# Two-layer streaming encoder on one core: the layer-2 operand ring shrunk to four tiles when attention opens, output weights loaded into the freed room, and block 0's products dealt over eight chunks

## Chip, cores, metric

One core of a Trainium2 chip runs the program. The metric is the device time of one execution in microseconds. Of the kernel before there are three timed runs and one profiled execution.

## What is computed

The reference is one step of an encoder of two layers on a prompt of 2048 tokens and a sample of 32, width 1024, in fp32. Layer 1 is a gated delta rule with a short convolution, an output projection and a layer norm. Then keys and values are projected once, and layer 2 is attention over a sliding window of three chunks of 64 tokens, with a learned sink for each of its 16 heads (four to a key head of 64):

```python
def swa_layer(x, k, v, pos, cached, w_in, sinks, w_out, ln_g, ln_b):
    proj = x @ w_in
    q = rope_partial(proj[..., :B_QW].reshape(b, l, B_Q_HEADS, B_HD), pos) * (B_HD ** -0.5)
    z = proj[..., B_QW:]
    o = cached_attention(q, k, v, sk) if cached else banded_attention(q, k, v, sk)
    out = (o * jax.nn.silu(z)) @ w_out
    return layer_norm(DN_ALPHA * x + out, ln_g, ln_b)
...
    s = jnp.einsum('bnqkgd,bnskd->bnkgqs', qb, kb)
    p = sink_softmax(s, sinks)
    o = jnp.einsum('bnkgqs,bnskd->bnqkgd', p.astype(v.dtype), vb)
```

The change concerns only the passage from the products `x @ w_in` and `x @ w_kv` to this attention.

## The kernel before

The program runs in stages: layer 1's products, the delta rule, layer 1's output, the products of layer 2 (class `P2`), and attention (class `Attention`). Every fp32 product is made of three matmuls on operands split into a high and a low part.

**Layer 2's products.** The 2080 tokens are five blocks of 416. Blocks 1 to 4 are multiplied in pairs by a seven-product scheme (`winograd`, matmuls `ps<-xs_h,w` in the trace); block 0 is multiplied plainly (`plain`, L1259 to L1277, matmuls `ps<-x_h,w`). A unit is one of q, k, v or z and an index; a plain unit has four products, each of 12 matmuls (L1232 to L1234, 128x416), whose weights are one tile `w` of 512 KB. `load` (L1205 to L1215) keeps up to RING = 12 such tiles ahead, by DMAs issued on ScalarE (ACT). After two products, ACT scales the sum out of PSUM (L1271, tile `a`), VectorE (DVE) rotates it, and SyncE (SP) stores it to a buffer in HBM: `s_bk`, `s_bv`, `s_bq`, `s_bz` (L1371, L1358).

**Attention.** `load_kv(a, z)` fetches the keys `kT` and values `vd` of chunks a to z-1 on SP (L1423, L1429: one and four DMAs). `chunk(n)` handles 64 queries in two halves. A half is: scores S (L1565), their maximum on DVE (L1440, L1441), four exponentials on ACT (L1448), the sink's exponential (L1450), the sum on DVE (L1451, L1452), a scale of P on GpSimd (POOL, L1573), six transposes (L1580), copies `pt` on ACT (L1582) and DVE (L1584), and the value product `ot` (L1586), which DVE multiplies by the gate. Queries `qs` and gates `zs` come by SP (L1546, L1547) for each second chunk. `finish` (L1455 to L1494) is the output projection of 128 tokens, 48 matmuls `po` with the output weights `wo` (L1473 to L1475) and a layer norm; `flush(keep)` lets all but `keep` of the finished pairs through it. These matmuls can stand between the steps of a half.

**The passage.** `program` runs chunks 10 to 31 and then 0 to 9. In four rounds, four plain products are written, then a chunk, then a `load_kv`. The 16 products at stake are the last four units of `sequence` (q1, q2, q3, v of block 0). When they are done the right side of SBUF, ring included, is closed, and `open_right` loads the output weights, 8 MB in 16 DMAs of 512 KB on SP (L955). Up to the end of `P2`'s large part the order on the engines is written out by hand; in the attention the framework's scheduler chooses it from the dependences. An engine runs its own list strictly in that order. The build hands each DMA of SP and of ACT one of eight completion counters (DMAHW0 to DMAHW7) in turn, and the issuing engine waits until the previous DMA with that counter has landed.

Of the kernel before, what the change touches and what calls it, by code (L numbers as in the profile page):

```python
# [10 lines left out]
F32 = mybir.dt.float32  # L11
F32R = mybir.dt.float32r
# [7 lines left out]
D = 1024  # L20
# [137 lines left out]
def drain(gen):  # L158
    for _ in gen:
        pass  # L160
# [926 lines left out]
class P2:  # L1087
# [10 lines left out]
    def __init__(self, tc, right, mid, I, O, T, G):  # L1098
        self.tc, self.nc, self.I, self.O, self.T, self.G = tc, tc.nc, I, O, T, G
        self.res = new_pool(tc, right, "p2_res", 1, side="right")  # L1100
        self.wp = new_pool(tc, right, "p2_w", self.RING, side="right")
        self.wk = new_pool(tc, right, "p2_wk", 3, side="right")
        self.stg = new_pool(tc, mid, "p2_stg", 3, side="right")
        self.ppr = new_pool(tc, right, "p2_psr", 2, PSUM, side="right")
        self.ppl = None
        self.turn = 0
        self.todo, self.second, self.staged = [], [], []
# [99 lines left out]
    def load(self, most=2):  # L1207

        for _ in range(most):
            if self.loads and len(self.held) < self.RING:  # L1210
                what, slot = self.loads.pop(0)
                w = self.wp.tile([128, 2, 4, 128], F32R, tag="w", name="w")
                src = self.T["w2"][UNITS.index(what[:2]), SLOTS.index(slot)]
                self.nc.scalar.dma_start(w[:].rearrange("p s k c -> p s (k c)").bitcast(F32), src)
                self.held.append((what, slot, w))  # L1215

    def weight(self, what, slot):
        whose, which, w = self.held.pop(0)
# [160 lines left out]
class Attention:  # L1379


    def __init__(self, tc, left, I, O, T, G):
        self.tc, self.nc, self.I, self.O, self.T, self.G = tc, tc.nc, I, O, T, G
        nc, V = tc.nc, tc.nc.vector
        L = "left"
        self.one = one = new_pool(tc, left, "t_one", 1, side=L)
        self.two = new_pool(tc, left, "t_two", 2, side=L)
        self.thr = new_pool(tc, left, "t_thr", 3, side=L)
        self.ps_s = [new_pool(tc, left, "t_ps", 1, PSUM, side=L)]
        self.ps_t = new_pool(tc, left, "t_pt", 2, PSUM, side=L)  # L1390
        self.ps_o = new_pool(tc, left, "t_po", 1, PSUM, side=L)
        self.turn = 0
        self.kT = one.tile([128, 2, NP], F32, tag="kT", name="kT")

        self.vd = one.tile([128, 32, 2, 128], F32, tag="vd", name="vd")
        self.nsk = one.tile([128, 8], F32, tag="nsk", name="nsk")
        self.sks = one.tile([128, 4], F32, tag="sks", name="sks")
        for i in range(2):
            nc.sync.dma_start(self.nsk[i * 64:i * 64 + 64, :], I["sinks"][i].partition_broadcast(64))
        for i in range(4):  # L1400
            nc.sync.dma_start(self.sks[i * 32:i * 32 + 32, :], I["sinks_s"][i].partition_broadcast(32))
        V.tensor_scalar(out=self.nsk[:], in0=self.nsk[:], scalar1=-1.0, scalar2=None, op0=ALU.mult)
        V.tensor_scalar(out=self.sks[:], in0=self.sks[:], scalar1=-1.0, scalar2=None, op0=ALU.mult)
        self.pend = []
        self.data = {}

    def open_right(self, right):
        tc, I = self.tc, self.I
        R = "right"
        self.oone = new_pool(tc, right, "u_one", 1, side=R)  # L1410
        self.otwo = new_pool(tc, right, "u_two", 2, side=R)
        self.pp = new_pool(tc, right, "u_pp", 1, PSUM, side=R)
        self.ps_s.append(new_pool(tc, right, "u_ps", 1, PSUM, side=R))
        rest = load_out_weights(self.nc, self.oone, self.T["wo"][1])
        self.w = next(rest)
        drain(rest)

    def tables(self):
        self.tabs = ln_tables(self.nc, self.oone, self.I["b_ln_g"], self.I["b_ln_b"])
# [196 lines left out]
def program(tc, I, O, T, G):  # L1616
    nc = tc.nc
    left, right, mid = ExitStack(), ExitStack(), ExitStack()
# [51 lines left out]
    pairs = [("v", 0), ("z", 0), ("k", 0), ("z", 1), ("q", 0), ("z", 2), ("q", 1), ("z", 3), ("q", 2), ("q", 3)]  # L1670
    sequence = [("z", j, 0) for j in range(3)] + [p + (1,) for p in pairs]
    sequence += [("z", 3, 0), ("k", 0, 0), ("q", 0, 0)] + [p + (2,) for p in pairs]
    sequence += [("q", j, 0) for j in range(1, 4)] + [("v", 0, 0)]
    first, second = Filler(gated()), Filler(outputs())

    def done(ch):
# [24 lines left out]
    p2.ppl = None  # L1701
    left.close()
    mid.close()
    att = Attention(tc, left, I, O, T, G)
    att.load_kv(8, 14)
    order = list(range(10, 32)) + list(range(10))
    for i in range(4):
        drain(itertools.islice(late, 4))
        att.chunk(order.pop(0))
        if i != 2:  # L1710
            att.load_kv(*{0: (14, 18), 1: (18, 24), 3: (24, 32)}[i])
    drain(late)
    p2.rest()
    right.close()
    att.open_right(right)
    att.load_kv(0, 8)
    for n in order:
        att.chunk(n)
        if n == 15:
            att.tables()  # L1720
        if n == order[-1]:
            att.flush(1)
            att.pend.insert(0, None)
            att.pend.pop(0)
            att.sample()
            att.pend.reverse()
        if n % 2 == 1:
            att.flush(3 if n < 24 and n > 9 else 2)
# [142 lines left out]
```

## Time and profile before

| | us |
|---|---|
| profiled execution | 2252.59 (span 2250.8) |
| timed runs | 2246.57, 2263.61, 2265.81 (median 2263.61) |
| last Winograd matmul starts | 1805.8 |
| first keys issued | 1813.31 |
| first scores start | 1824.43 |
| output weights issued | 1841.9 to 1859.9 |
| first output product starts | 1881.1 |
| granted TensorE clock, mean | 0.979 |

Times are from the start of the span. In the views, PE is TensorE's matmul, PEld its weight load, and a name with a q behind it (SPq, ACTq) is an engine's queue of DMA issues. `[7.30 <-DMA w<-s_w]` behind a row says that the engine had been idle 7.30 us and what ended that. A row of the table by stretch gives start and end, length, busy time and count of each engine, the granted clock, the share of the DMA engines and GB/s.

### The profile page before, as it was taken

What the parts mean: (1) busy time and instruction counts of PE and PEld (TensorE: products, weight loads), DVE (VectorE), ACT (ScalarE), POOL (GpSimd) and SP (SyncE); (2) the same over time, 40 slices, a digit from 0 to 9 for tenths busy, and PEclk for the clock granted to TensorE, in tenths of its full rate; (3) what the DMA queues carried; (4) which work ended last, traced back from release to release, by engine and by line L of the source; (5) the groups of instructions that cost most, each with busy time, mean ns of one, the idle gap of its engine ahead of it and who ended that gap; (6) DMA issues with size and microseconds to landing.
All of it is one profiled execution on the core that took longest, in us unless ns stands there. A gap on an engine that the chain in (4) does not pass through costs nothing. (4 is left out here: it accounts for less than half of the span.)

```text
span 2250.8 us, 37045 instructions
## 1 busy us (share of the span) xinstructions
PE 2152.2 (96%) x13370; PEld 1959.0 (87%) x13370; DVE 1470.4 (65%) x2701; ACT 902.7 (40%) x2331; POOL 740.9 (33%) x1193
## 2 busy tenths in 40 slices
PE   8999999999999999999889999899989998999997
PEld 6899999999998889988777787899989986888775
DVE  4798777876484577777655665545844566556662
ACT  4555555444332466656552211311311135444441
POOL 1213111251112387777661210000000024656563
PEclk9999999999999899999999999999999999999999
DMA  7656656567734334435724874888788896233321
GB/s 285 211 185 194 193 179 197 183 193 235 235 117 130 113 117 138 148 114 171 277 75 157 285 224 148 284 279 290 249 297 291 266 286 183 85 104 94 85 80 43
DMA packets 344919, 417.40 MB, mean 185 GB/s; under 512 B 77968, under 2 KB 275696, under 8 KB 344720
## 3 DMA queue, kind: packets, MB, share of 16 engines
q1 hardware_dynamic: 312432, 314.41, 44.1%
q10 hardware_dynamic: 32304, 100.62, 13.4%
q8 instruction: 106, 1.74, 0.3%
q14 instruction: 77, 0.63, 0.1%
HBM read 265.26 MB, written 150.05 MB: 185 GB/s over the span
## 5 line engine op out<-in xcount | busy, mean ns | idle before, releaser
L77 PE MATMUL ps<-act_hi,w_hi 128*128 128x416 f32 x1280 | 459.3, 359 | 6.4 <-ACT R L297 4.3
L79 PE MATMUL ps<-act_hi,w_lo 128*128 128x416 f32 x1280 | 451.7, 354 | 5.2 <-POOL w_lo L54 5.2
L78 PE MATMUL ps<-act_lo,w_hi 128*128 128x416 f32 x1280 | 451.8, 353 | 0.0
L77 PEld LDWEIGHTS ps<-act_hi,w_hi 128*128 128x128 f32 x1280 | 242.4, 189 | 11.2 <-ACT R L297 4.6
L79 PEld LDWEIGHTS ps<-act_hi,w_lo 128*128 128x128 f32 x1280 | 242.7, 190 | 9.7 <-POOL w_lo L54 6.3
L78 PEld LDWEIGHTS ps<-act_lo,w_hi 128*128 128x128 f32 x1280 | 243.2, 190 | 2.7
L54 POOL TENSOR_TENSOR w_lo<-w_raw,w_hi 128x1024 fp32r<-128x1024 f32 x40 | 101.5, 2537 | 381.5 <-ACT w_hi L53 374.9
L1232 PE MATMUL ps<-xs_h,w 128*128 128x416 f32 x560 | 199.4, 356 | 10.9 <-DVE ra L1289 6.9
L1233 PE MATMUL ps<-xs_l,w 128*128 128x416 f32 x560 | 199.9, 357 | 2.9 <-DVE xs_l L1135 2.9
L1234 PE MATMUL ps<-xs_h,w 128*128 128x416 f32 x560 | 198.2, 354 | 0.0
L266 DVE SCALAR_TENSOR_TENSOR y<-R,convw,y 128x2083 f32<-128x2083 f32 x72 | 171.2, 2379 | 24.5 <-ACT y L264 24.4
L559 POOL TENSOR_TENSOR tm<-L,Tt 128x60 f32<-128x60 f32 (+19 forms) x375 | 132.1, 352 | 86.3 <-DVE tm L559 34.1
L562 POOL TENSOR_TENSOR Tt<-Tt,tm 128x60 f32<-128x60 f32 (+19 forms) x375 | 143.4, 382 | 28.5
L1573 POOL TENSOR_TENSOR P<-P,sm 128x384 f32<-128x384 f32 (+2 forms) x128 | 101.0, 810 | 122.5 <-DVE sm L1452 59.1
L1427 POOL MEMSET vd<- 64x768 f32 (+2 forms) x10 | 7.8, 779 | 395.9 <-DVE ra L1289 395.6
L1448 ACT ACTIVATE P<-S,nm 128x192 f32<-128x192 f32 (+2 forms) x260 | 104.8, 419 | 61.4 <-DVE nm L1441 48.9
L1232 PEld LDWEIGHTS ps<-xs_h,w 128*128 128x128 f32 x560 | 106.3, 190 | 13.8 <-DVE ra L1289 7.6
L1289 DVE SCALAR_TENSOR_TENSOR ra<-ps,u 128x416 f32<-128x416 f32 x60 | 35.4, 590 | 122.0 <-PE ps L1234 121.2
L1008 PE MATMUL po<-wo,g_hi 128*128 128x512 f32 (+1 forms) x272 | 110.5, 406 | 3.0 <-DVE r L1013 1.8
L1010 PE MATMUL po<-wo,g_lo 128*128 128x512 f32 (+1 forms) x272 | 107.5, 395 | 4.5 <-DVE g_lo L995 4.5
L1233 PEld LDWEIGHTS ps<-xs_l,w 128*128 128x128 f32 x560 | 106.1, 189 | 5.5 <-DVE xs_l L1135 4.2
L1234 PEld LDWEIGHTS ps<-xs_h,w 128*128 128x128 f32 x560 | 106.9, 191 | 1.2
(292 smaller groups left out, 4808.7 us busy)
## 6 DMA issues: line engine op xcount, KB each, us to landing
w<-s_w ACTq DMA_DIRECT2D x180, 512.0 KB
s_w<-pre_hl SPq DMA_DIRECT2D x160, 256.0 KB
w_raw<-in_w_in SPq DMA_DIRECT2D x40, 512.0 KB
s_wo<-pre_hl SPq DMA_DIRECT2D x64, 256.0 KB
wo<-s_wo SPq DMA_DIRECT2D x32, 512.0 KB
gb<-s_gcum SPq DMA_DIRECT2D x34, 256.0 KB
k<-s_k SPq DMA_DIRECT2D x34, 256.0 KB
s_z<-z SPq DMA_DIRECT2D x40, 208.0 KB
```

The source lines that it names most:

```text
L77: nc.tensor.matmul(ps, hi[:, k, :], xh[:, k, :], start=(k == 0), stop=False)
L78: nc.tensor.matmul(ps, hi[:, k, :], xl[:, k, :], start=False, stop=False)
L79: nc.tensor.matmul(ps, lo[:, k, :], xh[:, k, :], start=False, stop=(k == KC - 1))
L266: nc.vector.scalar_tensor_tensor(out=y[:], in0=R[:, j:j + W], scalar=self.convw[:, i, j:j + 1], in1=y[:], op0=ALU.mult, op1=ALU.add)
L559: P.tensor_tensor(out=tm[:n, i0 - k:, :w], in0=L[:n, i0:, j:j + 1].to_broadcast(sh), in1=Tt[:n, j:j + 1, :w].to_broadcast(sh), op=ALU.mult)
L562: P.tensor_tensor(out=Tt[:n, i0:, :w], in0=Tt[:n, i0:, :w], in1=tm[:n, i0 - k:, :w], op=ALU.subtract)
L1008: nc.tensor.matmul(ps[:n], ghi[:, k, :n], w[0][k][:, cs], start=(k == 0), stop=False)
L1010: nc.tensor.matmul(ps[:n], glo[:, k, :n], w[0][k][:, cs], start=False, stop=(k == KC - 1))
L1232: nc.tensor.matmul(ps, w[:, 0, k], xh[:], start=first and k == 0, stop=False, skip_group_check=True)
L1233: nc.tensor.matmul(ps, w[:, 0, k], xl[:], start=False, stop=False, skip_group_check=True)
L1234: nc.tensor.matmul(ps, w[:, 1, k], xh[:], start=False, stop=last and k == 3, skip_group_check=True)
L1448: nc.scalar.activation(P[u], src, AF.Exp, bias=nm[:, u:u + 1], scale=1.0, accum_out=sm[:, u:u + 1])
```

## The change

The pools of `P2` swap places, so that the ring is the last opened and can be closed alone. When the Winograd part is over, `smaller` closes the ring of 12 and opens one of 4. The four tail units are no longer in `sequence`: they start behind that, by `p2.units(tail)`, whose first step loads four tiles. The output weights are now eight tiles of 1 MB. Seven go into a new pool `t_w` of the left side, one written after each of the first seven chunks; the eighth comes with `open_right`. Eight rounds of a chunk, an output weight, two plain products and (in rounds 0, 1 and 3) a `load_kv` take the place of four rounds. The layer-norm tables are loaded behind `open_right` instead of behind chunk 15, and `flush(3)` is called once before chunk 18.

```diff
@@ class P2
-        self.wp = new_pool(tc, right, "p2_w", self.RING, side="right")
         self.wk = new_pool(tc, right, "p2_wk", 3, side="right")
+        self.ring = ExitStack()
+        self.wp = new_pool(tc, self.ring, "p2_w", self.RING, side="right")
...
+    def smaller(self, right):
+
+        assert not self.held and not self.loads
+        self.ring.close()
+        self.RING = 4
+        self.wp = new_pool(self.tc, right, "p2_w4", self.RING, side="right")
@@ class Attention
+        self.wpool = new_pool(tc, left, "t_w", 1, side=L)
+        self.wo = []
...
-        rest = load_out_weights(self.nc, self.oone, self.T["wo"][1])
-        self.w = next(rest)
-        drain(rest)
+        self.out_weight(self.oone)
+        self.w = [[w[:, s] for w in self.wo] for s in range(2)]
+
+    def out_weight(self, pool):
+
+        k = len(self.wo)
+        w = pool.tile([128, 2, D], F32R, tag=f"wo{k}", name="wo")
+        self.nc.sync.dma_start(w[:].bitcast(F32), self.T["wo"][1, k])
+        self.wo.append(w)
@@ program
-    sequence += [("q", j, 0) for j in range(1, 4)] + [("v", 0, 0)]
+    tail = [("q", j, 0) for j in range(1, 4)] + [("v", 0, 0)]
...
+    p2.smaller(right)
     att = Attention(tc, left, I, O, T, G)
     att.load_kv(8, 14)
+    late = p2.units(tail)
+    next(late)
     order = list(range(10, 32)) + list(range(10))
-    for i in range(4):
-        drain(itertools.islice(late, 4))
+    for i in range(8):
         att.chunk(order.pop(0))
-        if i != 2:
+        if i < 7:
+            att.out_weight(att.wpool)
+        drain(itertools.islice(late, 2))
+        if i in (0, 1, 3):
             att.load_kv(*{0: (14, 18), 1: (18, 24), 3: (24, 32)}[i])
     drain(late)
     p2.rest()
     right.close()
     att.open_right(right)
+    att.tables()
     att.load_kv(0, 8)
+    att.flush(3)
     for n in order:
         att.chunk(n)
-        if n == 15:
-            att.tables()
```

Up to the end of the Winograd part the engines run the same lists, except that block 0's 38 early plain matmuls are gone from PE. Three places behind it differ in what the prediction speaks of. In the rows, the number behind a name is the tile's, and the bracket lists what the instruction waits for: the counters above, and the engines' own semaphores.

ACT, where the plain products end and the softmax begins. Before:

```order
L1214 DMA w_17760<-s_w2_73 128x1024 [waits DMAHW2_49,PE_49]
L1271 ACTIVATE a_17745<-ps_17716 128x416 [waits DMAHW6_49,DVE_49]
L1214 DMA w_17778<-s_w2_73 128x1024 [waits DMAHW4_49,PE_49]
L1271 ACTIVATE a_17780<-ps_17747 128x416 [waits DMAHW1_49,DVE_49]
L1271 ACTIVATE a_17899<-ps_17870 128x416 [waits DMAHW3_49,DVE_49,PE_49]
L1271 ACTIVATE a_17932<-ps_17903 128x416 [waits DMAHW1_49,DVE_49,PE_49]
L1271 ACTIVATE a_18045<-ps_18016 128x416 [waits DMAHW1_49,DVE_49,PE_49]
L1448 ACTIVATE P_17796,sm_17800<-S_17791,nm_17797 128x3x64 [waits DVE_49,PE_49]
```

and with the change:

```order
L1215 DMA w_17932<-s_w2_73 128x1024 [waits DMAHW7_49,DMAHW2_49,PE_49]
L1279 ACTIVATE a_17934<-ps_17901 128x416 [waits DVE_49]
L1215 DMA w_18039<-s_w2_73 128x1024 [waits DMAHW3_49,DMAHW0_49,PE_49]
L1464 ACTIVATE P_17719,sm_17723<-S_17714,nm_17720 128x3x64 [waits DVE_49,PE_49]
L1464 ACTIVATE P_17719,sm_17723<-S_17714,nm_17720 128x3x64 x3
L1466 ACTIVATE es_17724<-es_17724 128x4 [waits DVE_49]
L1215 DMA w_18057<-s_w2_73 128x1024 [waits DMAHW5_49,PE_49]
L1279 ACTIVATE a_18059<-ps_18026 128x416
L1215 DMA w_18151<-s_w2_73 128x1024 [waits DMAHW6_49,DMAHW1_49,PE_49]
L1598 COPY pt_17735<-tr_17736 128x384 [waits PE_49]
```

The last weight load (`w_17778`) stood ahead of every exponential. Now the ninth weight (`w_18039`) stands ahead of the first one, the tenth and eleventh (`w_18057`, `w_18151`) ahead of the first copy `pt`. The counter DMAHW3 that the ninth waits for was last given to the sixteenth `vd` on SP, DMAHW5 of the tenth and DMAHW6 of the eleventh to the sixth and seventh output tiles.

SP, where the first output tiles and the first keys go out, with the change:

```order
L1431 DMA wo_17786<-s_wo_74 128x2048 [waits DMAHW4_49]
L1379 DMA s_bq_69<-ra_17602 128x416 [waits DMAHW5_49,DVE_49]
L1431 DMA wo_17899<-s_wo_74 128x2048 [waits DMAHW7_49]
L1431 DMA wo_18024<-s_wo_74 128x2048 [waits DMAHW1_49]
L1379 DMA s_bq_69<-ra_17557 128x416 [waits DMAHW3_49,DVE_49]
L1431 DMA wo_18136<-s_wo_74 128x2048 [waits DMAHW4_49,PE_49]
...
L1439 DMA kT_17677<-s_bk_71 128x2x384 [waits DMAHW4_49,PE_49]
```

Before, the row ahead of that `kT` was a load of the sinks, and every `wo` stood behind the last keys. Now four tiles stand ahead of the first keys: the fourth waits, by DMAHW4, for the first to land, and `kT`, by the same counter, for the fourth.

SP, behind the last of the values that the eight rounds fetch, with the change:

```order
L1445 DMA vd_17678<-s_bv_72 64x8x64 [waits DMAHW2_49]
L1445 DMA vd_17678<-s_bv_72 64x8x64 [waits DMAHW3_49]
L1431 DMA wo_18261<-s_wo_74 128x2048 [waits DMAHW4_49]
L1431 DMA wo_18373<-s_wo_74 128x2048 [waits DMAHW5_49,PE_49]
L1431 DMA wo_18491<-s_wo_74 128x2048 [waits DMAHW6_49]
L1439 DMA kT_17677<-s_bk_71 128x2x512 [waits DMAHW7_49]
```

Before, the store of a query block and then this `kT` followed on the values. Now the fifth, sixth and seventh output tiles stand between.

## Prediction

> **What bounds the kernel now.** I read the page first, then the table by stretch, because a share over the whole span hides where an engine idles.
>
> ```profile
> span 2250.8 us, 37045 instructions
> PE 2152.2 (96%) x13370; PEld 1959.0 (87%) x13370; DVE 1470.4 (65%) x2701; ACT 902.7 (40%) x2331; POOL 740.9 (33%) x1193
> ```
> ```profile
> core 0: us, PE busy (x) PEld busy (x) DVE busy (x) ACT busy (x) POOL busy (x), PEclk, DMA share, GB/s
> 1806.00:1841.00 35.00, 35.00 (x200) 32.96 (x199) 23.36 (x56) 9.14 (x32) 9.90 (x13) 1.00 1.00 245
> 1841.00:1881.00 40.00, 29.38 (x162) 21.52 (x161) 23.10 (x56) 19.77 (x85) 12.99 (x17) 0.87 1.04 327
> 1886.00:2200.00 314.00, 313.55 (x1715) 249.29 (x1714) 192.33 (x462) 145.20 (x559) 186.92 (x175) 1.00 0.30 85
> ```
> TensorE (PE) bounds the program. It is full while block 0's products fill it (1806 to 1841) and again once output products fill it (from 1886); between, some nine halves of chunks run with nothing beside them, and PE idles 40.00 - 29.38 = 10.6 us at a granted clock of 0.87 (29.38 us of work at 0.87 is worth 25.6 at full clock, 3.8 lost; at the most 40 x 0.13 = 5.2). So about 16 us is all that this change can win here, and 16 of 2252.6 is 0.7%. What releases the output products, by the view of the tile `wo` and the waits:
>
> ```profile
> L955 SPq DMA_DIRECT2D wo<-s_wo x16: 319/320/580, 1841.9 to 1859.9; - x16
> L1473 PE MATMUL po<-wo,g_hi x13: 388/392/775, 1881.1 to 1898.0; 128*128 128x512 f32 x13
> its engine sat idle before it (us, times) until:
>   issue: 0.7, 2
>   DVE pt L1584: 0.2, 1
> ```
> ```profile
> POOL P L1573 <- DVE sm L1452: 29.9, 7, 8.0
> ACT P L1448 <- DVE nm L1441: 13.1, 5, 3.9
> PE S L1565 <- ACT P L1448: 7.6, 5, 2.5
> ```
> The output weights are issued until 1859.9 and the first output product starts at 1881.1, and nothing waits for them there. The bare halves wait on themselves: scores, maximum (DVE), exponential (ACT), scale (POOL), transposes.
>
> **The change part by part.** *Work moved out of the Winograd part.* By the order on PE, 38 of the 192 matmuls of the 16 products stand before the last Winograd matmul now, and none afterwards.
>
> ```profile
> L1234 PE MATMUL ps<-xs_h,w x68: 348/352/355, 1760.2 to 1805.8; 128*128 128x416 f32 x68
> L1232 PEld LDWEIGHTS ps<-x_h,w x14: 186/188/188, 1778.1 to 1805.9; 128*128 128x128 f32 x14
> ```
> A matmul goes at the pace of its weight load, 0.188 us, so a product of 12 takes 2.26 us and the Winograd part ends 38 x 0.188 = 7.1 us sooner, at 1798.6. PE's work up to the first output product is the same 192 matmuls and 12 scores.
>
> *Weights of the tail.* Each product loads one 512 KB tile. Now the last load is issued at 1808.02 (below), before any exponential; afterwards four go out as the Winograd part ends and twelve in turn, each behind a product, on ACT's queue among the exponentials. On SP four 1 MB output tiles go out ahead of the first keys, and three behind the keys of chunks 24 to 31, ahead of those of chunks 0 to 7. The order shows each DMA waiting for one of eight counters that SP and ACT share, that is, for an earlier DMA to land. That such a wait holds the engine, the trace shows:
>
> ```profile
> 1798.75 7.71 ACTq L1214 DMA_DIRECT2D w<-s_w  x5
> 1806.56 0.52 ACT L1271 ACTIVATE a<-ps 128x416 f32<-128x416 f32 x1 [7.30 <-DMA w<-s_w]
> 1808.02 0.33 ACTq L1214 DMA_DIRECT2D w<-s_w  x1
> ```
> ```profile
> SPq L955 <- DMA wo<-s_wo: 9.0, 9, 1.6
> ACT vb L1356 <- DMA s_bv<-va: 3.7, 1, 3.7
> ```
> ACT stood 7.30 us behind the landing of a weight, and SP 9.0 us in nine waits behind its own tiles. (The Trainium skill, "DMA: Bandwidth & Descriptors", section "Anatomy of one DMA — SWDGE (gpsimd) path", says that DMA engines wait on no semaphore and the wait stands on the issuing sequencer; these rows agree. Were the wait held in the queue instead, ACT would go on to its exponentials and the sum would be that of the first rival.)
>
> *First keys.* `kT` of the first chunks waits for the fourth output tile, which waits for the first. The Winograd part's end lets the first three go at about 1796.5 (their place on SP is that of the stores that start at 1800.12 now, less what of the 7.1 us lies before them).
>
> ```profile
> 1800.12 7.84 SPq L1371 DMA_DIRECT2D s_bq<-ra  x3
> 1813.31 0.39 SPq L1423 DMA_DIRECT2D kT<-s_bk  x1
> 1813.80 2.64 SPq L1429 DMA_DIRECT2D vd<-s_bv  x4
> 1817.14 1.16 SPq L1546 DMA_DIRECT2D qs<-s_bq  x2
> 1833.30 3.41 SPq L1429 DMA_DIRECT2D vd<-s_bv  x4
> 1841.86 1.29 SPq L955 DMA_DIRECT2D wo<-s_wo  x3
> ```
> ```profile
> 1849.00:1865.00 16.00, 11.72 (x64) 8.59 (x63) 9.99 (x24) 6.95 (x32) 5.23 (x7) 0.89 1.03 407
> ```
> Four tiles (4.2 MB), five weights (2.6 MB) and three stores (0.6 MB) are 7.4 MB; at the 407 GB/s of 1849 to 1865, when tiles were loading, 18.2 us: the first keys are issued at about 1815 (at the 327 GB/s of the whole stretch 1841 to 1881, 22.6 us and 1819). Now it is 1813.31, but PE had products until then. Queries go out 3.8 to 5 us after the keys and land by the 3.7 us of `vb`'s row, so the first scores can start at about 1823, while PE has finished the five products ahead of them at 1798.6 + 5 x 2.26 = 1809.9. That idles PE 13 us.
>
> *Exponentials behind the ninth weight.* On ACT the ninth weight stands ahead of the first exponential and waits, by its counter, for the sixteenth `vd`. In the rows above that last `vd` is issued 1836.71 - 1813.31 = 23.4 us after the first keys, and 3.7 us more land it: 27 us, so 1815 + 27 = 1842. The bounds: 28 transfers at the 0.39 us of `kT` plus 3.7 is 15 us (1830); 28.5 us from first keys to first `wo` plus 3.7 is 32 (1847). I take 27, since the same 28 instructions gave it. Behind the ninth weight wait the softmax of the first half, the tenth weight (for the sixth output tile) and the eleventh (for the seventh), and behind that the first `pt` copy, for which PE waits with `ot`. The three output tiles go out at about 1840: 3.1 MB and a weight at 407 GB/s are 9 us, landing included 3.7: 1849 to 1853; I take 1851.5 for PE's restart. By then it has done seven products and two scores and one set of transposes.
>
> *What is left then*, with prices from the chain and the time line:
>
> ```profile
> 1909.86 1.29 PE ot L1586 x6
> 1911.16 0.66 PE tr L1580 x6
> 1911.81 0.85 PE S L1565 x8
> ```
> ```profile
> 1837.70 0.60 PE L1354 MATMUL ps<-ident,a 128*128 128x128 f32 x4
> 1858.49 1.61 POOL L1573 TENSOR_TENSOR P<-P,sm 128x384 f32<-128x384 f32 x2 [3.09 <-DVE sm L1452]
> 1863.08 1.61 POOL L1573 TENSOR_TENSOR P<-P,sm 128x384 f32<-128x384 f32 x2 [2.98 <-DVE sm L1452]
> ```
> Nine products 9 x 2.26 = 20.3, ten scores 8.5, nine transposes 5.9, ten `ot` 12.9, two value transposes 1.2: 48.8 us. A half is 1.29 + 0.66 + 0.85 = 2.8 us of PE and a bare one comes each 1863.08 - 1858.49 = 4.6, so 1.8 is lost in each; six or seven remain bare (nine now): 11.7. The first output product would start at 1851.5 + 60.5 = 1912, against 1881.1. It stands one transpose and two `ot` later in the order than now, 0.66 + 2 x 1.29 = 3.2 us of work already done: 1912 - 1881.1 - 3.2 = +27.7, so **+28 us**. From there PE has 313.55 of 314 us in work and the same work in both, so the delay stays to the end. The two table loads, which move ahead, cost nothing, since SP has no other load that PE waits for by then; uncovered they are
>
> ```profile
> ln_g<-in_b_ln_g SPq DMA_DIRECT2D x1, 512.0 KB
> ```
> twice 512 KB, 2.6 us at 407 GB/s.
>
> The profiled execution took 2252.6 us (span 2250.8), so its time would be 2280.6. The three timed runs lie at 2246.6, 2263.6 and 2265.8; the mean of these and the profiled one is 2257, and with +28 I forecast **2285 us**, 0.9% above the median shown.
>
> **The rivals.** *The room pays (on the other side).* If the `vd` landed before the first scores were needed, or the counters came round in another state, ACT would not be held. PE's work from 1798.6: 16 products 36.2, twelve scores 10.2, ten transposes 6.6, ten `ot` 12.9, value transposes 1.2 are 67.1, plus 11.7 for bare halves: 1877.4, less 3.2: -7 us, **2250**. It decides if the first queries land by 1810 and the sixteenth `vd` within a product or two after, which asks for the keys 13 us sooner than 7.4 MB allow; 407 GB/s against it is strong. For it speaks only that the counter's turn is taken from the build, and the landing of a tile from a rate.
> *Only the keys are late.* The ninth weight goes out early, since the `vd` are quick (15 us) and PE is idle until 1823 in any case: -7 + 13 = +6, **2263**. Against it: with 15 us after 1815 ACT is still held until 1830.
> *Longer and colder.* At 289 GB/s instead of 407
>
> ```profile
> GB/s 298 302 268 175 81 248 231 254 275 238 282 286 222 257 237 309 275 188 274 317 212 334 348 412 391 413 415 386 418 419 415 389 293 110 232 337 250 274 215 281
> DMA packets 27800, 21.68 MB, mean 289 GB/s; under 512 B 17414, under 2 KB 24658, under 8 KB 27794
> 1881.00:1886.00 5.00, 5.00 (x22) 3.57 (x21) 4.20 (x7) 3.39 (x17) 5.00 (x3) 0.67 1.15 304
> ```
> the mean of 1806 to 1881, the 7.4 MB take 25.6 us (7.4 later) and the last three tiles 3.6 later: +39, **2296**. The granted clock of 0.67 after PE's idling (1881 to 1886) adds 5 x 0.33 = 1.7 us per long gap. (The Trainium skill, "TensorE: Matmul & The Clock Gate", Part 1, halves the clock after an idle window of about 3.4 us and restores it after as long a busy one, an estimate of 1.7 us a gap; the 0.67 agrees, and two gaps would make +31 of +28.)
> *The change does not do what it says.* Room for the output weights is opened before attention, but the eighth tile still waits for the ring's end and three more stand behind the keys of chunks 24 to 31. Since no output product waited for `wo` in the rows above, that moves neither sum; it only means that nothing repays the delay.
>
> **How the numbers follow.** About 1%, 22.6 us, is what a measurement of this kernel can tell from no change. The forecast (+28, on its own +16 to +37 by the bounds of the `vd`, of the rate and of the bare halves) has 0.60; the room pays 0.15; only the keys 0.12; longer and colder 0.13. Slower by over 1% is 0.7 of the forecast's 0.60 and all of the last: 0.55; faster by over 1% asks for more than the whole 16 us and gets 0.03; the rest, 0.42, is within 1%. Range: 2256 (nearly down to the room paying) to 2306 (longer and colder, with 10 us for the spread of runs).
>
> **What would show it.** Right: the first `kT` issued at 1813 to 1821, PE idle before the first scores; ACT with a weight load on its queue that waits from about 1812 to 1842 and no exponential before; PE idle over 20 us in 1810 to 1852, bare halves six or seven; first output product at 1905 to 1920, and 313 to 314 busy of 314 us behind it. Wrong: exponentials before 1835, or a first output product before 1890, which would leave the first rival; or a tail of the program that is not full, which would let the delay be won back.

## Result and the profile after

| | before | change |
|---|---|---|
| median, us | 2260.48 (4 runs, 2246.57 to 2265.81) | 2307.14 (4 runs, 2303.38 to 2317.72) |
| profiled execution, us (span) | 2252.59 (2250.8) | 2303.38 (2301.6) |
| ratio of the times | | 1.0236, 95% interval 1.0206 to 1.0266 |

The change makes the kernel 2.4% slower, some 47 to 53 us (difference of the medians; 0.0236 of 2257). The forecast was +28 us, with 2306 as the upper end of the range. The ratios in this document leave out three single executions of 3499.79 to 4223.98 us, far above all others; one of them is the only profiled execution of the last experiment, so no row of that one is used.

To compare the two executions they must start together. The first Winograd matmul of before, then of the change (instruction, count, duration in ns, first and last start in us):

```profile
L1232 PE MATMUL ps<-xs_h,w x560: 349/352/714, 1428.9 to 1805.4; 128*128 128x416 f32 x187
```
```profile
L1240 PE MATMUL ps<-xs_h,w x560: 345/348/716, 1434.0 to 1803.8; 128*128 128x416 f32 x187
```

The change is 5.1 us late there, so 45.7 of the 50.8 us of span arise behind that point. Below, times of the change less 5.1 are put beside those of before. Of the 5.1 us, 4.1 belong to the change as well: from the last `op<-Sp,q` matmul of the delta rule (L711, at 1207.7 and 1208.7) to the first Winograd matmul it is 221.2 us before and 225.3 with the change. The swapped pools show in between: the first weight tile of layer 2 is issued 15 us behind that `op` instead of 18, and this is so in every trace with the swapped pools (eleven, with the experiments below) and in none of the five with the old ones. Layer 1's output then waits longer for its own load `r`. Waits from 1225 to 1262 us (who waited for whom: us in total, times, longest), before and then the change:

```profile
PE po L1008 <- DVE r L1013: 1.8, 1, 1.8
DVE r L1013 <- DMA r<-in_x: 0.7, 1, 0.7
```
```profile
PE po L1008 <- DVE r L1013: 4.4, 2, 2.6
DVE r L1013 <- DMA r<-in_x: 4.8, 1, 4.8
```

Over all traces the way from that `op` to the first Winograd matmul is 225.1 to 227.9 us with the swapped pools and 221.2 to 225.6 with the old ones. That the earlier weight loads delay `r` fits these rows, but no run swaps the pools alone.

The table by stretch of the change, with the header of the one before:

```profile
1804.40:1833.00 28.60, 15.52 (x61) 14.12 (x59) 6.82 (x15) 0.52 (x1) 6.32 (x9) 0.72 0.97 313
1833.00:1863.00 30.00, 11.33 (x48) 9.52 (x48) 7.58 (x21) 3.68 (x15) 1.61 (x2) 0.64 1.11 318
1863.00:1927.00 64.00, 55.76 (x311) 44.30 (x309) 29.75 (x81) 26.04 (x109) 14.95 (x19) 0.97 0.47 143
1932.00:1996.00 64.00, 62.46 (x312) 48.42 (x313) 36.87 (x74) 23.75 (x87) 32.70 (x30) 0.97 0.30 85
```

In the first 58.6 us behind the Winograd part PE works 26.85 us and idles 31.8, at a granted clock of 0.72 and 0.64. Before, the first 35 us of that place had no idle time. ACT's row of time shows who was late (start, duration, instruction; in brackets the idle time ahead and its end; an ACTq row of several issues lasts from the first to the last of them, waits included):

```profile
1800.05 28.06 ACTq L1215 DMA_DIRECT2D w<-s_w  x6
1828.21 0.52 ACT L1279 ACTIVATE a<-ps 128x416 f32<-128x416 f32 x1 [27.70 <-DMA vd<-s_bv]
1829.46 8.63 ACTq L1215 DMA_DIRECT2D w<-s_w  x2
1838.13 0.52 ACT L1279 ACTIVATE a<-ps 128x416 f32<-128x416 f32 x1 [9.40 <-DMA vd<-s_bv]
1852.83 0.33 ACTq L1215 DMA_DIRECT2D w<-s_w  x1
1853.26 0.42 ACT L1464 ACTIVATE P<-S,nm 128x192 f32<-128x192 f32 x1 [14.61 <-DMA vd<-s_bv]
1858.22 0.33 ACTq L1215 DMA_DIRECT2D w<-s_w  x1
1858.59 0.52 ACT L1279 ACTIVATE a<-ps 128x416 f32<-128x416 f32 x1 [3.53 <-DMA wo<-s_wo]
1861.80 0.33 ACTq L1215 DMA_DIRECT2D w<-s_w  x1
1862.17 0.48 ACT L1598 COPY pt<-tr 128x384 f32<-128x384 f32 x1 [3.06 <-PE tr L1596]
```

ACT does almost nothing from 1800.5 to 1853. Its first six weight loads take 28.06 us; in narrower windows they go out like this:

```profile
1800.05 1.29 ACTq L1215 DMA_DIRECT2D w<-s_w  x3
1807.54 0.33 ACTq L1215 DMA_DIRECT2D w<-s_w  x1
1821.73 0.33 ACTq L1215 DMA_DIRECT2D w<-s_w  x1
1827.78 0.33 ACTq L1215 DMA_DIRECT2D w<-s_w  x1
```

So ACT stands from the fifth weight on: 13.8 us until, by the trace's semaphore events, a load of the sinks (`sks`) has landed, which SP issues behind the fourth output tile, and the sixth weight 5.6 us more until a `vd` has. The eighth waits for a `vd` again, and the ninth until 1852.83, for the sixteenth `vd`. Everything behind stands: the drains of the products (`a`), and the exponentials. The tenth weight goes when an output tile has landed (the `wo` in brackets). SP at the same time:

```profile
1801.75 0.70 SPq L1431 DMA_DIRECT2D wo<-s_wo  x1
1804.43 0.98 SPq L1431 DMA_DIRECT2D wo<-s_wo  x2
1809.87 0.32 SPq L1431 DMA_DIRECT2D wo<-s_wo  x1
1820.85 0.40 SPq L1439 DMA_DIRECT2D kT<-s_bk  x1
1835.10 0.34 SPq L1379 DMA_DIRECT2D s_bq<-a  x1
1843.48 1.11 SPq L1379 DMA_DIRECT2D s_bq<-a  x1
1845.11 2.61 SPq L1445 DMA_DIRECT2D vd<-s_bv  x4
1847.77 2.59 SPq L1431 DMA_DIRECT2D wo<-s_wo  x3
```

Four output tiles, then the first keys at 1820.85. Two stores of the products (`s_bq<-a`) stand between the keys and values. ACT drains these products late (1828.21 and 1838.13), but SP did not wait for that: DVE is done with them at 1831.1 and 1841.2, 4.0 and 2.3 us before the stores go out. SP's waits from 1832 to 1840 us are for its own transfers:

```profile
SPq L1379 <- DMA zs<-s_bz: 2.4, 1, 2.4
SPq L1445 <- DMA kT<-s_bk: 1.3, 1, 1.3
```

PE:

```profile
1816.42 0.72 PE L1240 MATMUL ps<-x_h,w 128*128 128x416 f32 x1 [5.11 <-DMA w<-s_w]
1828.78 0.72 PE L1240 MATMUL ps<-x_h,w 128*128 128x416 f32 x1 [7.97 <-ACT a L1279]
1833.24 1.35 PE L1581 MATMUL S<-kT,qs 64*128 64x192 f32 x8
1855.03 1.65 PE L1581 MATMUL S<-kT,qs 64*128 64x192 f32 x8 [17.99 <-ACT P L1464]
1862.70 1.56 PE L1602 MATMUL ot<-pt,vd 128*128 128x256 f32 x6 [0.68 <-ACT pt L1598]
```

It waited 5.11 us for a weight, 7.97 for a drain and 17.99 for the first exponential, which frees the only bank of scores. The matmul behind the first two waits took 0.72 us and not the 0.35 of the rows around it. The granted clock behind the three waits is 0.5 for 4.1, 5.4 and 6.5 us of renewed work (until 1820.5, 1834.2 and 1861.5). (The Trainium skill, "TensorE: Matmul & The Clock Gate", Part 1, says that an idle array falls to half its clock and gets it back after at least one busy window of some 3.4 us; the 0.72 against 0.35 agrees with the half, and the three times are one to two such windows.) The first output product of the change:

```profile
L1489 PE MATMUL po<-wo,g_hi x23: 389/393/628, 1927.0 to 1959.8; 128*128 128x512 f32 x23
```

### The profile page after: what moved, and what is told of

It is laid out like the page before. It is cut to its first block, busy times and chain, and to the rows that moved or that the text cites. A ratio compares the mean times of both kernels' runs of the same rounds, so it can differ in the third digit from the quotient of the medians.

```text
span 2301.6 us, 37032 instructions
## 1 busy us (share of the span) xinstructions
PE 2165.5 (94%) x13370; PEld 1964.8 (85%) x13370; DVE 1473.9 (64%) x2701; ACT 904.3 (39%) x2331; POOL 744.1 (32%) x1193
## 3 DMA queue, kind: packets, MB, share of 16 engines
q10 hardware_dynamic: 32304, 100.62, 13.1%
## 5 line engine op out<-in xcount | busy, mean ns | idle before, releaser
L1240 PE MATMUL ps<-xs_h,w 128*128 128x416 f32 x560 | 198.9, 355 | 11.7 <-DVE ra L1297 7.7
L1240 PEld LDWEIGHTS ps<-xs_h,w 128*128 128x128 f32 x560 | 106.5, 190 | 15.3 <-DVE ra L1297 8.4
L1602 PE MATMUL ot<-pt,vd 128*128 128x256 f32 x372 | 100.3, 393 | 7.7 <-DVE pt L1600 4.7
```

What stands on the lines that cost most here:

```text
L1240: nc.tensor.matmul(ps, w[:, 0, k], xh[:], start=first and k == 0, stop=False, skip_group_check=True)
L1602: nc.tensor.matmul(ot[:, p], self.vd[:, kc0 + j, p, :], pt[:, 2 * j:2 * j + 2, :], start=(j == 0), stop=(j == nj - 1))
```

## Experiments

All ratios are to the kernel before, run on the same chip. "Scores" and "output" are the start of the first scores and of the first output product, counted from the first Winograd matmul of the same execution.

| run | ratio (95%) | scores | output |
|---|---|---|---|
| before | 1 | 395.5 | 452.2 |
| the change | 1.0236 (1.0206 to 1.0266) | 399.2 | 493.0 |
| e1_late_wo | 1.0153 (1.0110 to 1.0195) | 391.5 | 489.6 |
| e2_pool_w | 1.0129 (1.0088 to 1.0171) | 403.8 | 474.4 |
| e3_both | 1.0058 (1.0035 to 1.0081) | 390.0 | 478.0 |
| e4_deal | 1.0062 (1.0040 to 1.0084) | 397.0 | 437.4 |
| e5_tables | 0.9997 (0.9966 to 1.0028) | 396.5 | 445.4 |
| e6_nodeal | 1.0253 (1.0211 to 1.0296) | 397.7 | 494.2 |
| e7_nodeal_free | 1.0095 (1.0061 to 1.0130) | 390.2 | 468.1 |
| e8_deal6 | 1.0022 (0.9997 to 1.0047) | 396.8 | 455.0 |
| e9_ring8 | 1.0142 (1.0102 to 1.0182) | 423.6 | 463.3 |
| e10_ring8_keep | 1.0073 (1.0046 to 1.0100) | 412.6 | 461.4 |
| e11_ring12_keep | 1.0028 (1.0008 to 1.0047) | 402.5 | 442.2 |
| e12_before_wo_pool | 1.0050 (1.0027 to 1.0072) | 397.0 | 455.9 |
| e13_ring8_pool | 1.0084 (1.0052 to 1.0116) | 405.9 | 459.2 |
| e14_ring8_keep_pool | 1.0044 (1.0021 to 1.0066) | 397.3 | 453.1 |
| e15_ring12_keep_pool | 0.9995 (0.9974 to 1.0016) | | |

**Undoing one hold at a time.** The theory after the result: two holds, the first keys behind four output tiles, and ACT behind weight loads. Rival A: the ring of four is too short in itself. Rival B: the keys alone. Rival C: the dealing.

`e1_late_wo`, the seven output tiles pinned behind the last values:

```diff
@@ load_kv
-                nc.sync.dma_start(self.vd[rows, a:z, p, rows], src[:, a:z, p, rows])
+                self.last = nc.sync.dma_start(self.vd[rows, a:z, p, rows], src[:, a:z, p, rows])
@@ program
-        if i < 7:
-            att.out_weight(att.wpool)
...
+    with tc.issue_after(att.last.ins):
+        for _ in range(7):
+            att.out_weight(att.wpool)
     drain(late)
```

> The change with one thing put back: the seven output tiles go out on SP behind the last keys and values of the eight rounds instead of four of them ahead of the first keys. The ring of four and its loads on ACT stay. Theory (two holds: the first keys stand behind four output tiles, and ACT stands with a weight load behind a counter that a late transfer of SP must give back): the first hold is gone and the second shorter, since the values land some 10 us sooner; first keys at 1808 to 1813, first exponential 1825 to 1840, time 2260 to 2285, so over half of the 47 us is won back. Rival A (the short ring alone costs it: each weight is fetched too late): 2295 to 2310. Rival B (the keys alone): 2252 to 2262.

It took 2295.88 us, less than half of the loss back, so the theory's number failed, and rival B with it; it lies at the lower edge of rival A's range, which the next runs tell apart. The trace shows why, in ACT's and PE's rows of this run:

```profile
1834.88 0.42 ACT L1464 ACTIVATE P<-S,nm 128x192 f32<-128x192 f32 x1 [0.79 <-DVE nm L1457]
1878.09 0.33 ACTq L1215 DMA_DIRECT2D w<-s_w  x1
1878.46 0.52 ACT L1279 ACTIVATE a<-ps 128x416 f32<-128x416 f32 x1 [17.05 <-DMA wo<-s_wo]
```
```profile
1880.65 1.65 PE L1581 MATMUL S<-kT,qs 64*128 64x192 f32 x8 [16.58 <-ACT P L1464]
```

The first exponential came early (395.9 us from the first Winograd matmul, 419.3 in the change), but now the last weight load waited 17.05 us for an output tile to land, and the exponentials behind it with PE for 16.58 us. The hold on ACT had not gone; it had moved to where the output tiles were put.

`e2_pool_w`, the weights of the tail by GpSimd, whose transfers have counters of their own in the order:

```diff
@@ load
-                self.nc.scalar.dma_start(w[:].rearrange("p s k c -> p s (k c)").bitcast(F32), src)
+                self.queue.dma_start(w[:].rearrange("p s k c -> p s (k c)").bitcast(F32), src)
@@ __init__
         self.ring = ExitStack()
+        self.queue = self.nc.scalar
@@ smaller
         self.RING = 4
+        self.queue = self.nc.gpsimd
```

> The change with one thing put back: the sixteen weight loads of the tail are issued by GpSimd, whose transfers have counters of their own, so ACT holds no transfer among its exponentials. Four output tiles still stand ahead of the first keys. Theory: the first exponential follows the first scores within 3 us (about 1835), the 20 us in which ACT stood are gone, the late keys stay: 2265 to 2285. Rival B (the keys alone): no gain, 2300 to 2310. Rival A (short ring): no gain, 2295 to 2310.

2289.18 us: four us outside the theory's range, but neither rival's. The exponential follows on the scores by 2.9 us (406.7 against 403.8). The run is not the clean half that was meant: in its order all seven output tiles go out ahead of the first keys and not four, so the keys come at 396.6 us (386.8 in the change), and the gain by GpSimd is, if anything, understated:

```profile
1800.47 0.44 SPq L1433 DMA_DIRECT2D wo<-s_wo  x1
1803.15 2.23 SPq L1433 DMA_DIRECT2D wo<-s_wo  x4
1806.55 3.40 SPq L1433 DMA_DIRECT2D wo<-s_wo  x2
```

What is left shows mainly in one row, PE's wait for the queries that follow the late keys:

```profile
1837.77 1.65 PE L1583 MATMUL S<-kT,qs 64*128 64x192 f32 x8 [25.46 <-DMA qs<-s_bq]
```

`e3_both` joins the two edits.

> Both of the above at once: weights of the tail by GpSimd, output tiles behind the last keys. Theory: both holds are gone; within 10 us of the kernel before, 2250 to 2270. Rival A (short ring): 2285 to 2310, since each weight is still fetched only four ahead.

2274.66 us, so 0.0058 of the 0.0236, some 13 us, stay: the theory's number fails by 5 us and something of rival A is there. One wait is most of it, in PE's row (the swapped pools, too, are still in this run):

```profile
1829.12 1.65 PE L1583 MATMUL S<-kT,qs 64*128 64x192 f32 x8 [10.63 <-DMA qs<-s_bq]
```

The order of this run puts four products (48 matmuls) ahead of the first scores, where before 98 stood there; keys, then queries, still need their 13 us (377.1 to 390.0), and PE, with none of its 16 products in the Winograd part, is through with these four 10.63 us sooner.

**The other parts alone.** `e4_deal`: the kernel before with the eight rounds.

```diff
-    for i in range(4):
-        drain(itertools.islice(late, 4))
+    for i in range(8):
         att.chunk(order.pop(0))
-        if i != 2:
+        drain(itertools.islice(late, 2))
+        if i in (0, 1, 3):
...
     att.open_right(right)
+    att.tables()
     att.load_kv(0, 8)
+    att.flush(3)
...
-        if n == 15:
-            att.tables()
```

> The kernel before with the dealing alone: ring of 12, block 0's tail in the sequence, output weights as before in sixteen transfers by the open right side, but eight rounds of a chunk and two products instead of four of four products and a chunk, and the tables and one flush placed as in the change. Theory: the dealing costs nothing by itself: 2252 to 2268. Rival C (the dealing spreads products so that the halves of the chunks get less cover and the later order is worse): 2285 to 2310.

2273.48 us, beyond the theory's range and short of the rival's. The first output product came 14.8 us sooner than before, and the way from there to the end is 27.5 us longer (397.2 against 369.7), part of which is work that the kernel before does ahead of its first output product (1970 matmuls stand behind that product here, 1908 before). 9.5 us of it are idle time of PE: 397.20 - 375.58 = 21.6 against 12.1.

`e5_tables`, the tables' place alone:

```diff
     att.open_right(right)
+    att.tables()
     att.load_kv(0, 8)
...
-        if n == 15:
-            att.tables()
```

> The kernel before with the tables alone placed as in the change (loaded behind the output weights instead of behind chunk 15); ring, weights and four rounds as before. By the order this alone makes the scheduler cut the later part finer (three transposes, then output products, where six stood together). Theory D (part of the 15 us that remained with both holds gone is this finer order): 2264 to 2275, with the first output product within 5 us of before and the loss behind it. Rival C (the dealing itself): 2253 to 2263.

2257.63 us against 2256.91, the other range: theory D fell. The first output product came 6.8 us sooner and the rest took 7.3 us more. The scheduler's finer order of the later part, which this run has, costs nothing that could be measured.

`e6_nodeal`, the change with four rounds of four products ahead of a chunk and no early flush; `e7_nodeal_free`, the same with the edits of e1 and e2:

```diff
-    for i in range(8):
+    for i in range(4):
+        drain(itertools.islice(late, 4))
         att.chunk(order.pop(0))
-        if i < 7:
+        for _ in range(2 if i < 3 else 1):
             att.out_weight(att.wpool)
-        drain(itertools.islice(late, 2))
-        if i in (0, 1, 3):
+        if i != 2:
...
-    att.flush(3)
```

> The change without the dealing: ring of four, weights on ACT, output tiles by SP early, but four rounds of four products and a chunk, and no early flush. Theory (two holds, 32 us, and some 15 us by the dealing and the later order): the holds stay, so 2285 to 2305, and the first exponential stays some 20 us behind the first scores. Rival C (the dealing is what makes the holds): 2255 to 2270.

> The change without the dealing and with both holds taken away: ring of four, its weights by GpSimd, output tiles behind the last keys, four rounds of four products and a chunk, no early flush. By the order the later part is cut as in the kernel before. Theory: nothing is left that costs, 2250 to 2266. Rival A (the short ring): 2270 to 2290.

Without the dealing the holds are as large as with it, 2313.16 us (8 above the range), and the first exponential comes 27.4 us behind the first scores: rival C is out as their cause. The second missed: 2279.1, in rival A's range. Its PE has the same wait as e3's ahead of the first scores:

```profile
1832.83 1.65 PE L1583 MATMUL S<-kT,qs 64*128 64x192 f32 x8 [10.90 <-DMA qs<-s_bq]
```

`e8_deal6`: the kernel before with 3, 3, 3, 3, 2, 2 products behind six chunks.

> The kernel before with the 16 products dealt over six chunks (3, 3, 3, 3, 2, 2), ring of 12 and output weights as before, no early flush, tables behind the output weights. If the dealing itself is good for cover (a first output product 15 us earlier was seen with eight) and the flush is what costs: 2245 to 2258. Theory D (the finer later order eats it): 2262 to 2278.

2261.18 us, within a few us of before, on neither range's side: the first output product is not sooner (455.0) and nothing is won.

**A longer ring.** Here the ring that `smaller` opens is 8 or 12, and fewer output tiles go early, so that both fit:

```diff
-        self.RING = 4
+        self.RING = 8
...
-        if i < 7:
+        if i < 4:
             att.out_weight(att.wpool)
...
-        self.out_weight(self.oone)
+        while len(self.wo) < 8:
+            self.out_weight(self.oone)
```

> The change with two sizes altered: a ring of eight tiles instead of four, and four early output tiles of 1 MB instead of seven; the other four go out when the right side opens. By the order all sixteen weight loads on ACT then stand ahead of the first exponential and ten products instead of five ahead of the first scores; the four output tiles still stand ahead of the first keys. Theory (three terms: the cover that the short ring takes from the first scores, the late keys, ACT held among its exponentials): the first and third go, the late keys stay and are mostly covered by ten products (22 us): 2258 to 2275. If the late keys cost 14 us by themselves whatever stands ahead: 2272 to 2282. If only the dealing over eight chunks is left: 2268 to 2278.

2300.13 us: every expectation missed. No exponential stands behind a weight load any more, and ten products stand ahead of the scores; but ACT's drains of those products stand behind the loads:

```profile
1809.09 27.01 ACTq L1215 DMA_DIRECT2D w<-s_w  x9
1836.22 0.52 ACT L1279 ACTIVATE a<-ps 128x416 f32<-128x416 f32 x1 [26.62 <-DMA sks<-in_sinks_s]
```
```profile
PE ps L1240 <- ACT a L1279: 18.5, 3, 8.1
```

Of the waits of PE in this stretch, 18.5 us are for drains. The `sks` in brackets is the small load of the sinks behind the output tiles on SP. `e10_ring8_keep` pins each early tile in its written place, behind the first keys:

```diff
-        self.nc.sync.dma_start(w[:].bitcast(F32), self.T["wo"][1, k])
+        self.tc.keep_in_program_order(self.nc.sync.dma_start(w[:].bitcast(F32), self.T["wo"][1, k]))
```

> As the run before, but the four early output tiles keep their written places on SP, behind the first keys and between the later ones. Theory: none of the three terms is left; it stands at what the dealing over eight chunks with the ring of 12 gave (2273) or a little below, 2255 to 2273. If the keys' place costs nothing once there is cover, the same as the run before.

2280.26 us, 20 below the run before, and 7 above the range: the drains still stand behind weights, for 11.0 us instead of 18.5:

```profile
PE ps L1240 <- ACT a L1279: 11.0, 3, 5.8
```

`e11_ring12_keep`, with a ring of twelve and three early tiles:

> Ring of twelve (closed and opened again, so without the early prefetch), three early output tiles in their written places, the rest when the right side opens; eight rounds. Tells whether more room for the ring than eight is worth anything: theory, twelve products ahead of the first scores are more than are needed, the same as with eight within 8 us, 2255 to 2273.

2266.07 us, 14 below the ring of eight, more than the 8 expected.

`e12_before_wo_pool`, the sixteen output-weight loads of the kernel before on GpSimd's queue instead of SP's:

```diff
-            nc.sync.dma_start(w[:, k, s].bitcast(F32), src[k, :, s])
+            (nc.gpsimd if nc_late else nc.sync).dma_start(w[:, k, s].bitcast(F32), src[k, :, s])
...
-        rest = load_out_weights(self.nc, self.oone, self.T["wo"][1])
+        rest = load_out_weights(self.nc, self.oone, self.T["wo"][1], True)
```

> The kernel before with one thing changed: its sixteen output-weight loads are issued by GpSimd instead of SP, so queries and stores on SP don't stand behind them and the landing counters of SP and ACT are free. If the bare halves of the kernel before wait on SP's queue: 2235 to 2250. If they wait only on their own chain of scores, maximum, exponential and scale, as its waits say: 2252 to 2264.

2275.87 us, slower, on neither side. The first output product came at 455.9 (452.2 before) and the rest took 11.5 us more, in an order that the scheduler cut finer. Two rows hold most of the loss, ACT's and PE's:

```profile
1874.73 0.26 ACT L1356 COPY vb<-ps 32x128 f32<-32x128 f32 x1 [20.14 <-DMA s_bv<-va]
1876.64 1.65 PE L1565 MATMUL S<-kT,qs 64*128 64x192 f32 x8 [21.17 <-ACT P L1448]
```

A copy on ACT waits 20.14 us for a store of values (`s_bv<-va`, issued on SP at 1853.02) to land while the output weights load, the exponentials stand behind it, and PE stands for 21.17 us. Between the first scores and the first output product PE idles 23.9 us here and 10.6 before. So this edit made a hold of the same kind on ACT, and it does not test whether the bare halves wait for SP's queue.

**The square.** Late or prompt keys by weights on ACT or GpSimd, all with a ring of eight, and the ring of twelve with neither hold. The edits are those of e2 and e10.

> The run with a ring of eight and four output tiles ahead of the first keys (2300), with the tail's weights issued by GpSimd. Theory (ACT's drain of the products stood behind weight loads for 18.5 us there): PE no longer waits for the drains, 2272 to 2290; the late keys stay. If the late keys alone made that run slow: 2293 to 2303.

> As the run before, but with the four output tiles in their written places behind the first keys: neither hold, and eight products ahead of the first scores. Theory: within 8 us of the kernel before or below it, 2245 to 2268. If the dealing over eight chunks costs 15 us whatever else stands: 2270 to 2282.

> Ring of twelve, three early output tiles in their written places, the tail's weights by GpSimd: no hold and more products ahead of the first scores. Theory: the first output product comes 10 to 15 us sooner than in the kernel before; if the later order gives nothing back, 2240 to 2256, else 2256 to 2268.

| ring | late keys, ACT | prompt keys, ACT | late keys, GpSimd | prompt keys, GpSimd |
|---|---|---|---|---|
| 4 | 1.0236 (change) | 1.0153 (e1) | 1.0129 (e2) | 1.0058 (e3) |
| 8 | 1.0142 (e9) | 1.0073 (e10) | 1.0084 (e13) | 1.0044 (e14) |
| 12 | | 1.0028 (e11) | | 0.9995 (e15) |

Prompt keys are the tiles behind the last values in e1 and e3, and in their written places in the rest; four tiles go early with a ring of eight, three with twelve. Late keys are four tiles ahead of the keys, but seven in e2. So the ring is not all that differs between two rows, nor the queue all that differs between the change and e2. Taking the weights off ACT is worth 0.0107 and 0.0095 with the ring of four (21 to 24 us), 0.0058 and 0.0029 with eight. Prompt keys are worth 0.0083 and 0.0071 (16 to 19 us), and 0.0069 and 0.0040. The intervals of the ratios leave each of these differences uncertain by 0.004 to 0.005 (an estimate from their half-widths), so the 0.0029 is not clear of nothing. With neither hold 0.0058 stay at four, 0.0044 at eight and nothing at twelve (interval 0.9974 to 1.0016); twelve is told from eight by this, four from eight is not. e13 came out at 2274.3, in its range; e14 at 2268.26, at the upper edge of its own; e15 at 2257.63, in the upper of its two ranges; whether its first output product came sooner, no trace shows. What the ring still costs where no hold is, shows in PE's wait for the first queries, in e14:

```profile
PE S L1584 <- DMA qs<-s_bq: 7.1, 1, 7.1
```

7.1 us here behind eight products, 10.63 in e3 behind four; e11, with twelve products ahead of the scores, has no such wait.

No version beat the kernel before. The best of the changed ones, e15, equals it.

## Why the prediction was wrong

The direction held, and the chain in the main: ACT behind weight loads, PE behind ACT. The size did not, 28 us against 49.8 in the trace, of which 45.7 lie behind the first Winograd matmul. The step that failed worst is the last one, that the delay stays as it is to the end; two more terms were too small, and one was put at nothing. Step by step:

- *"Up to the end of the Winograd part the engines run the same lists."* **A term put at nothing: +4.1 us.** With the swapped pools the first weight loads go out sooner and the first Winograd matmul comes 4.1 us later, by the rows above.
- *The Winograd part ends 7.1 us sooner.* 1804.2 less 5.1 is 1799.1 against 1805.8: 6.7. Right, counted from its start.
- *First keys at 1815.* 1820.85 less 5.1 is 1815.8. Right, but by luck, for two errors cancel: the first tile went 19.1 us ahead of the keys (forecast 18.2), and at the 313 GB/s of that stretch these are 6.0 MB, not 7.4 at 407.
- *First scores at 1823 with PE idle 13 us.* 1828.1, and the idle time was of another kind: 5.11 us for a weight and 7.97 for a drain behind the sixth weight load; that they add to 13.1 is chance. The forecast let ACT stand from the ninth weight on; it stood from the fifth, for a load of the sinks and then for values. The same hold, earlier, and on the drains as well.
- *The ninth weight at 1842, 27 us behind the first keys.* 1852.83 less 5.1 is 1847.7, or 32 us behind: the upper of the two bounds. I took 27 because "the same 28 instructions" had taken that long. They are not the same: the stretch before has 31 issues on SP, five of them stores, and the change's 28. These took 26.9 us all the same and not 23.4, since SP stood 2.4 and 1.3 us for its own `zs` and `kT` to land and an issue of `qs` took 2.6; and from the last `vd` to the ninth weight it was 5.1 us and not 3.7. **Mis-sized: +5.7 us**, of which 0.8 are the first keys'. It came through to PE's restart: 1857.6 instead of 1851.5, +6.1.
- *60.5 us from the restart to the first output product.* 64.3, **+3.8**. PE idled 8.2 of the 64 us of 1863 to 1927 (forecast 11.7), but was busy 55.8 instead of 48.8, with as many matmuls as the forecast lists (310; the row has 311): the prices were too low. They came from rows at full flow. Here, by the busy time of each tile (overlaps count for both), nine sets of transposes take 9.1 us (forecast 5.9), ten `ot` 17.2 (12.9), ten scores 10.0 (8.5) and the products with the value transposes 24.1 (21.5).
- *"From there PE has 313.55 of 314 us in work and the same work in both, so the delay stays to the end."* **This failed, by 8.1 us**: 3.2 us of lead were to come back, and instead the way from the first output product to the end is 374.6 us against 369.7. The stretch from the first output product to the end, in the change and before:

```profile
1927.00:2301.60 374.60, 357.17 (x1890) 276.22 (x1888) 222.19 (x494) 155.38 (x577) 213.33 (x193) 0.98 0.29 82
```
```profile
1881.10:2250.80 369.70, 357.62 (x1908) 278.88 (x1906) 212.11 (x500) 154.60 (x585) 213.09 (x193) 0.99 0.29 82
```

Idle time is 374.60 - 357.17 = 17.4 us against 12.1, 5.3 of the 8.1; the rest is work that took as long as before though there was less of it, at a clock of 0.98 and not 0.99. One of the waits, 6.3 us behind that product:

```profile
1933.30 2.08 PE L1602 MATMUL ot<-pt,vd 128*128 128x256 f32 x4 [3.38 <-DVE pt L1600]
```

The order shows that the later part is cut anew, and the prediction did not take that in. That a new order need cost nothing is shown by e5; which part of this one costs is open.

27.7 + 6.1 + 3.8 + 8.1 are the 45.7, and with the 4.1 of the first step they are 49.8; the last 1.0 of the 50.8 lies ahead of the delta rule's end.

Of the rivals, "the room pays" is out by the result, and in e15, where nothing holds, the room still wins nothing. "Only the keys" is out as a whole but stands as a term of 16 to 19 us with the ring of four. "The change does not do what it says" held in what it states: no output product waited for its weights in either execution. "Longer and colder" gave 2296, nearest to the result, for a wrong reason: the transfers moved 313 and 318 GB/s and the keys were on time; only its clock was right, 0.72 and 0.64 over 58.6 us. I had put the clock at 1.7 us for each long gap and left it out of the sum; half of the 4.1, 5.4 and 6.5 us at 0.5 is 8.0 us for three gaps, an estimate of 2.7 each.

A term had no price of its own: that the short ring takes cover from the first scores. The forecast had the idle time of 13 us ahead of them and let it go under in the hold of ACT. It comes to light when the holds are gone (0.0058 and 0.0095 in e3 and e7, nothing in e15), though in these numbers the swapped pools and the number of early tiles are not taken apart from the ring.

What stays open: why e4, with the ring of twelve and no hold, is 0.62% slower, when e15 deals over eight chunks too, with the same early flush, and loses nothing; and what the swapped pools cost alone.

## What to carry to other kernels

A load that is issued on a computing engine's queue is an instruction of that engine. When its issue has to wait for an unrelated transfer to land, all that is behind it waits, whether exponentials or drains; putting the big transfers elsewhere only chose another instruction to stand, and moving the loads to a queue with its own counters took the wait off that engine (e2, e3). It is no cure by itself: in e12 the output weights on such a queue came with a store that landed late, and ACT stood for 20.14 us behind that. So before a prefetch ring is made shorter, count how many of its loads will then be issued among the work of the next stage, and what each waits for.

Room that is opened for a transfer is worth only what waits for that transfer: no output product waited for its weights before, and no version here was faster for having them early.

## What the runs showed of the hardware

An engine that issues DMAs on counters shared with another queue can be held by that queue's transfers: ACT stood 13.8 us with a weight load until a load of the sinks on SP had landed, and until 1852.83 us for SP's sixteenth `vd`. (The Trainium skill, "DMA: Bandwidth & Descriptors", section "Anatomy of one DMA — SWDGE (gpsimd) path", puts a semaphore's wait on the issuing sequencer, not on the DMA engine; ACT's rows, and e2, in which ACT has no load to issue and its exponentials follow on the scores by 2.9 us, agree.) After gaps of 5.11, 7.97 and 17.99 us the granted clock was 0.5 for the first 4.1, 5.4 and 6.5 us of PE's work.
